# A 16x16 transpose of the identity between the down products and the next pair's gate and up products of an expert layer

## The chip, the cores and the metric

The kernel runs on one core of one Trainium2 chip. The metric is the device time of one execution in microseconds (us). Before the change the median of three runs is 2702.27 us (2701.55 to 2703.72).

## The reference, cut to what matters

The reference is one layer of a diffusion backbone over 2048 latent tokens of 1024 channels with 256 context tokens: a mixing sub-layer (a convolution beside an mLSTM scan), then a routed layer of 16 experts, then a final RMSNorm. The change lies in the routed layer alone. Each expert picks its 256 best tokens and runs them through a gated product of width 1408:

```python
aff = softmax(hs @ w_router, over experts)
g, idx = top_k(aff, cap)                    # cap = 256 tokens for each of 16 experts
xe = hs[idx]
a = einsum('ecd,edf->ecf', xe, w_gate)      # gate
u = einsum('ecd,edf->ecf', xe, w_up)        # up
ye = einsum('ecf,efd->ecd', silu(a) * u, w_down) * g[..., None]
out = segment_sum(ye, idx)                  # added back at the tokens' rows
```

All inputs are float32.

## The kernel before, in words

Each float32 operand of a large product is split into a rounded high part and a low part (`whi`, `wlo` for the weights, `xh`, `xl` for the tokens, `dhi`, `dlo` and `hh`, `hl` for the down product), and each product is the sum of three matmuls: high by high, high by low, low by high. ScalarE (ACT) makes the high parts and VectorE (DVE) the low parts, in lines 93, 97, 1075 and 1077.

The loop over the experts `e` (line 1157) holds a loop over `pr`, six pairs of 128-wide blocks of the 1408 hidden columns (the sixth pair has one block). For each pair the gate and up weights are loaded and split, and then for each block one PSUM tile `psx` takes the gate and the up product of 256 tokens: 2 x 8 x 3 = 48 matmuls with a moving operand of 256 columns, lines 1192 to 1194. A full pair so has 96 of them, called a run below, and the sixth pair 48. `psx` comes from the pool `pmm`, which has three buffers. ACT and DVE turn it into `hh` and `hl`.

The down products are one pair behind: after the gate and up products of pair `pr`, line 1212 issues those of the pair before, 24 matmuls (12 for a sixth pair) with 512 columns each into four PSUM accumulators `ac`, lines 1117 to 1119. Then, after pair 1, `xgather` finds the next expert's tokens with 16 small bf16 matmuls of 4 columns into `pi` (line 1013), and after pair 3 `xprep` transposes those tokens: 16 float32 transposes of 128x128 into `ptx` (line 1055), in four groups of four, which a planner spreads over the following pairs.

The order on each engine comes from a planner that works with modelled times. `keep_in_program_order` pins one instruction behind the last one written before it on the same engine. TensorE (PE) has a row of its own for the loading of stationary operands (PEld).

Of the kernel before, what the change touches and what calls it, by code (L numbers as in the profile page):

```python
# [8 lines left out]
F32 = mybir.dt.float32  # L9
# [10 lines left out]
P = 128  # L20
# [5 lines left out]
NE = 16  # L26
# [12 lines left out]
def kernel(ctx, tc, x, c, cx, c_ctx, w_mod, b_mod, g_norm1, g_norm2, w_in, w_out, conv_w, conv_b,  # L39
                       gate_b, g_head, w_router, w_gate_e, w_up_e, w_down_e, g_final, out):  # L40
    nc = tc.nc
    V, S, G, T = nc.vector, nc.scalar, nc.gpsimd, nc.tensor
# [20 lines left out]
    ident = con.tile([P, P], F32, name="ident")  # L63
# [20 lines left out]
    def load_w(src, rows, cols):  # L84
        raw = wrawp.tile([P, rows, cols], F32, name="wraw", tag="wraw")
        nc.sync.dma_start(raw, src)
        return raw
# [56 lines left out]
    def pool(st, name, bufs, **kw):  # L144
        return st.enter_context(tc.tile_pool(name=name, bufs=bufs, reuse_waits="tile", **kw))
# [3 lines left out]
    pmm = pool(left, "p1mm", 4, space=PSUM)  # L149
# [99 lines left out]
    for q in range(4):  # L249
        pmf = psm.tile([P, 512], F32, name="pm", tag="sm")  # L250
        pm = pmf[:, 0:8].rearrange("p (r i s) -> p r i s", r=2, i=2)
        for r in range(2):
            pr = pmm.tile([P, 512], F32, name="pr", tag="mm")
# [157 lines left out]
    def wstat(w, i, h, ntok):  # L411
        hi, lo = w
        his, los = h
        ps = pmm.tile([P, 512], F32, name="ps", tag="mm")
        for k in range(KD):
            wh = hi[:, k, i * P:(i + 1) * P]
            T.matmul(ps[:, :ntok], wh, his[k], start=k == 0, stop=False)  # L417
            T.matmul(ps[:, :ntok], wh, los[k], start=False, stop=False)  # L418
            T.matmul(ps[:, :ntok], lo[:, k, i * P:(i + 1) * P], his[k], start=False, stop=k == KD - 1)  # L419
        return ps  # L420
# [127 lines left out]
    for blk in range(4):  # L548
        KT = wk.tile([P, NH, 512], F32, name="KT", bufs=1)
        for j in range(2):  # L550
            w = wtile(2048 + j * 256)
            if blk == 0:
                for i in range(2):
                    ps = wstat(w, i, hc, NCTX)
                    S.activation(KTc[:, j * 2 + i, :], ps[:, :NCTX], AF.Copy)
            for i in range(2):
                ps = wstat(w, i, h, 512)
# [6 lines left out]
        for j in range(2):  # L564
            w = wtile(2560 + j * 256)
            if blk == 0:
                for t in range(2):
                    ps = hstat(w, hc, t)
                    V.tensor_copy(V1c[t][:, j * 2:j * 2 + 2, 0:P], ps[:, :256].rearrange("p (h v) -> p h v", h=2))
            for t in range(4):  # L570
                if j == 0:
                    V.memset(V1s[t][:, :, P:P + 1], 1.0)
                ps = hstat(w, h, t)
# [8 lines left out]
        for j in range(2):  # L582
            w = wtile(1536 + j * 256)
            for i in range(2):
                ps = wstat(w, i, h, 512)
# [60 lines left out]
        for j in range(2):  # L646
            mod_tile(j)
            w = wtile(3072 + j * 256)
            for t in range(4):
                so = wl.tile([P, 256], F32, name="so", bufs=2)  # L650
                ps = hstat(w, h, t)
# [4 lines left out]
        for j in range(2):  # L656
# [3 lines left out]
            for i in range(2):  # L660
                ps = wstat(w, i, h, 512)
# [5 lines left out]
            for i in range(2):  # L667
                ct = j * 2 + i
                ps = wstat(w, i, h, 512)
# [12 lines left out]
            for i in range(2):  # L682
                ct = j * 2 + i
                y = ys[i]
                ps = wstat(w, i, h, 512)
# [311 lines left out]
    with tc.tile_pool(name="xw", bufs=2, reuse_waits="tile") as xraw, tc.tile_pool(name="xh", bufs=2, reuse_waits="tile") as xhi, \  # L997
# [5 lines left out]
        def xgather(e):  # L1003
            oh = wk.tile([P, P, 16], BF16, name="oh", bufs=1)
            if e == 1:
                V.tensor_copy(oh[:, 0, 0:1], xp[1].bitcast(F32)[:, KD - 1, 0:1])
            for js in ((slice(0, 8), slice(8, 16)) if e == 0 else (slice(0, 16),)):
                n = js.stop - js.start
                V.tensor_tensor(oh[:, :, js], ix[:, :, js], AH[:, e, js].unsqueeze(1).to_broadcast([P, P, n]),
                                op=ALU.is_equal)  # L1010
            pi = ptr.tile([P, 512], F32, name="pi", tag="tr")
            for j in range(16):
                T.matmul(pi[:, 0:4], oh[:, :, j], RB[:, e, j], start=j == 0, stop=j == 15)
            idx = wk.tile([P, 2], I32, name="idx", bufs=3)
            with nc.allow_low_precision(reason="whole numbers up to 2047"):
                V.tensor_reduce(idx[:, ::-1], pi[:, 0:4].rearrange("p (h f) -> p h f", f=2), axis=AX.X, op=ALU.add)
            gxs = [wk.tile([P, XW], F32, name="gx", bufs=2) for _ in range(2)]
            for hf_ in range(2):
                G.indirect_dma_start(out=gxs[hf_], out_offset=None, in_=XN,
                                     in_offset=bass.IndirectOffsetOnAxis(ap=idx[:, hf_:hf_ + 1], axis=0))  # L1020
            if e == 0:
                warm = pmm.tile([P, 512], F32, name="warm", tag="mm")
                for j in range(20):
                    tc.keep_in_program_order(T.matmul(warm, oh[:, :, j % 16], ix[:, 0:32].rearrange("p a j -> p (a j)"),
                                                      start=True, stop=True))
            gg = wk.tile([P, 2], F32, name="gg", bufs=2)
            return gxs, gg, idx
# [74 lines left out]
        def early_store(t, a, fr):  # L1102
            V.scalar_tensor_tensor(a, a, fr, gfb, op0=ALU.mult, op1=ALU.mult)
            nc.sync.dma_start(out[t * P:(t + 1) * P, :], a)
# [48 lines left out]
                G.indirect_dma_start(out=out, out_offset=rows(e, hf_), in_=ar, in_offset=None)  # L1153

        xp = xprep(0, xgather(0))
        pend, held = [], []
        for e in range(NE):
            xh, xl, gg, idx = xp
            idx_of[e] = idx
            accs = None  # L1160
            nxt = None
            for pr in range(npair):
                n = 2 if pr < npair - 1 else NFT - 2 * (npair - 1)
                f0 = pr * 2
                ws = []
                for src in (w_gate_e, w_up_e):
                    raw = load_w(src[0, e][:, f0 * P:(f0 + n) * P].rearrange("(k p) n -> p k n", p=P), KD, n * P)
                    if e == 0 and pr == 0:
                        ws.append(split_w(raw, KD, n * P, thr[:, 0:1], nhalf))
                    elif e == 0 and pr == 1 and not ws:  # L1170
                        ws.append(split_w(raw, KD, n * P, xl.bitcast(F32)[:, 5, 0:1]))
                    else:
                        ws.append(split_w(raw, KD, n * P))
                dw = wsplit_d(w_down_e[0, e][f0 * P:(f0 + n) * P, :].rearrange("(i p) n -> p i n", p=P), n,
                              gg[:, 0:1] if e == 0 and pr < 2 else None,
                              xl.bitcast(F32)[:, KD - 1, 0:1] if e == 0 and pr < 2 else None)
                if e == 0 and pr == 0:
                    other_places(xl.bitcast(F32)[:, KD - 1, 0:1])
                for rec in held:
                    early_store(*rec)  # L1180
                held = []
                if e >= NE - 2 and pr:
                    cuts = ((0, 2, 4, 6, 8, 10), (10, 12, 14, 16, 16, 16))[e - NE + 2]
                    held = [early_load(t) for t in range(cuts[pr - 1], cuts[pr])]
                hts = []
                for i in range(n):
                    ps = pmm.tile([P, 2, 2 * P], F32, name="psx", tag="mm")
                    for m_ in range(2):
                        hi, lo = ws[m_]
                        for k in range(KD):  # L1190
                            wh = hi[:, k, i * P:(i + 1) * P]
                            T.matmul(ps[:, m_], wh, xh[:, k], start=k == 0, stop=False)  # L1192
                            T.matmul(ps[:, m_], wh, xl[:, k], start=False, stop=False)  # L1193
                            T.matmul(ps[:, m_], lo[:, k, i * P:(i + 1) * P], xh[:, k], start=False, stop=k == KD - 1)  # L1194
                    sgt = wk.tile([P, 2 * P], F32, name="sgt", bufs=2)
                    S.activation(sgt, ps[:, 0], AF.Silu)  # L1196
                    V.tensor_tensor(sgt, ps[:, 1], sgt, op=ALU.mult)  # L1197
                    if e == 0 and pr == 0 and i == 0:
                        wk.tile([P, 16], F32, name="gaph", bufs=1)
                    hh = wk.tile([P, 2 * P], F32R, name="hh", bufs=4)  # L1200
                    S.activation(hh, sgt, AF.Copy)  # L1201
                    hl = wk.tile([P, 2 * P], F32R, name="hl", bufs=4)
                    V.tensor_sub(hl, sgt, hh.bitcast(F32))
                    hts.append((hh, hl))
                last = pr == npair - 1
                for rec in held:
                    early_scale(rec, hts[-1][0].bitcast(F32)[:, 0:1])
                if pend and not (e == NE - 1 and last):
                    pe, pxp, paccs, ppr, plast = pend.pop()
                    if paccs is None:  # L1210
                        paccs = [pac.tile([P, 512], F32, name="ac", tag="ac") for _ in range(4)]
                    down(paccs, ppr)
                    if plast:
                        finish(pe, pxp, paccs)
                    else:
                        accs = paccs
                pend.append((e, xp, accs, ([f0 + i for i in range(n)], hts, dw), last))
                if e == NE - 2 and last:
                    old_rows(e)
                if pr == 1 and e + 1 < NE:  # L1220
                    gth = xgather(e + 1)
                if pr == 3 and e + 1 < NE:
                    nxt = xprep(e + 1, gth)
            if nxt is not None:
                xp = nxt
# [51 lines left out]
```

## Time and profile before

| what | value |
|---|---|
| median of three runs | 2702.27 us |
| time of the profiled execution | 2698.35 us |
| its span, first to last instruction | 2696.3 us |
| TensorE busy (PE) | 97% of the span |
| VectorE, ScalarE, GpSimd busy | 59%, 43%, 11% |
| gate and up matmuls (lines 1192 to 1194) | 8448, about 788 us busy each line |
| down matmuls (lines 1117 to 1119) | 2112, about 275 us busy each line |
| mean granted TensorE clock | 0.989 of full speed |

A matmul's duration in the profile reaches from its issue to its modelled end, and consecutive matmuls overlap. What a stream of them costs is therefore read from the distance between starts, or from the length of a stretch divided by the number of matmuls in it. In the window view the count in parentheses also takes in the two to four neighbours that reach into the stretch.

### The profile page before, as it was taken

To read this page: it belongs to the slowest core of one execution; us is meant where nothing else is said; L and a number is where in the kernel's file an instruction comes from. 1 tells how busy PE (TensorE), PEld (TensorE's weight loads), DVE (VectorE), ACT (ScalarE), POOL (GpSimd) and SP (SyncE) were. 2 spreads that over 40 slices of the span, in tenths; PEclk is the share of its full clock that TensorE was granted. 3 is DMA by queue.
4 is the path that set the end of the run, shared out by engine and by line. 5 is a ranking of instruction groups with operands and counts; after the bars stand their busy time and mean duration, and the time that the engine had idled before them with its cause. 6 is when DMAs were issued, how large, how long until landed. Compare 5 with 4: busy or idle time off the path is not lost.

```text
span 2696.3 us, 42922 instructions
## 1 busy us (share of the span) xinstructions
PE 2615.3 (97%) x17570; PEld 2365.0 (88%) x17570; DVE 1584.3 (59%) x2570; ACT 1155.3 (43%) x1723; POOL 301.0 (11%) x345
## 2 busy tenths in 40 slices
PE   8999999999999999689999999999999999999997
PEld 4988888888878888579999999999999999999987
DVE  5356454554575665566566556656655665665684
ACT  3243333422534444354444444444444444444553
POOL 1010000000111111210011011001101100110231
PEclk9999999999999999889999999999999999999999
DMA  8444554645656655165666666666666666666894
GB/s 271 135 147 148 170 165 147 196 129 156 204 183 206 208 183 172 64 219 188 205 217 208 200 209 219 189 208 214 209 202 208 219 191 206 214 210 202 276 318 166
DMA packets 382532, 524.57 MB, mean 195 GB/s; under 512 B 15072, under 2 KB 322736, under 8 KB 380288
## 3 DMA queue, kind: packets, MB, share of 16 engines
q1 hardware_dynamic: 327968, 437.96, 50.0%
q10 hardware_dynamic: 43792, 46.55, 5.1%
q0 software_dynamic: 10576, 37.32, 5.0%
q8 instruction: 138, 2.26, 0.3%
q14 instruction: 58, 0.48, 0.1%
HBM read 449.05 MB, written 72.61 MB: 193 GB/s over the span
## 4 chain that ended last, share of the span: by engine, by line
PE 63%; DMA 3%; DVE 2%; issue 2%; ACT 0%; POOL 0%; POOLq 0%; DVEq 0%; SPq 0%; ACTq 0%
PE psx L1192 12%; PE psx L1194 11%; PE psx L1193 11%; PE ac L1117 6%; PE ac L1119 6%; PE ac L1118 6%; PE po L730 2%; PE po L732 2%; PE po L731 2%; DMA pk<-PK 1%; PE ptx L1055 1%; PE pl L766 1%; PE pb L514 1%; PE pa L510 1%; DMA ACC<-yv,idx 1%
## 5 line engine op out<-in xcount | busy, mean ns | idle before, releaser
L1192 PE MATMUL psx<-xh,whi 128*128 128x256 f32 x2816 | 788.9, 281 | 1.6 <-ACT whi L93 1.5
L1193 PE MATMUL psx<-xl,whi 128*128 128x256 f32 x2816 | 786.7, 280 | 0.9 <-DVE xl L1064 0.9
L1194 PE MATMUL psx<-xh,wlo 128*128 128x256 f32 x2816 | 787.5, 280 | 0.0
L97 DVE TENSOR_TENSOR wlo<-wraw,whi 128x2048 fp32r<-128x2048 f32 x248 | 532.0, 2156 | 307.8 <-ACT whi L93 304.7
L93 ACT ACTIVATE whi<-wraw 128x2048 fp32r<-128x2048 f32 x248 | 446.7, 1804 | 373.3 <-PE psx L1193 112.1
L1194 PEld LDWEIGHTS psx<-xh,wlo 128*128 128x128 f32 x2816 | 535.3, 190 | 0.1
L1193 PEld LDWEIGHTS psx<-xl,whi 128*128 128x128 f32 x2816 | 530.5, 188 | 3.3 <-DVE xl L1064 1.4
L1192 PEld LDWEIGHTS psx<-xh,whi 128*128 128x128 f32 x2816 | 528.7, 188 | 4.1 <-ACT whi L93 1.7
L1117 PE MATMUL ac<-dhi,hh 128*128 128x512 f32 x704 | 276.2, 392 | 0.0
L1118 PE MATMUL ac<-dlo,hh 128*128 128x512 f32 x704 | 274.7, 390 | 0.0
L1119 PE MATMUL ac<-dhi,hl 128*128 128x512 f32 x704 | 273.3, 390 | 0.0
L1077 DVE TENSOR_TENSOR dlo<-draw,dhi 128x2048 fp32r<-128x2048 f32 x96 | 202.9, 2114 | 114.2 <-ACT dhi L1075 114.2
L418 PE MATMUL ps<-hlo,whi 128*128 128x512 f32 (+1 forms) x672 | 259.6, 387 | 0.0
L419 PE MATMUL ps<-hhi,wlo 128*128 128x512 f32 (+1 forms) x672 | 259.0, 386 | 0.0
L417 PE MATMUL ps<-hhi,whi 128*128 128x512 f32 (+1 forms) x672 | 258.6, 388 | 0.0
L1147 POOL DMA_INDIRECT ACC<-yv,idx x28 | 82.8, 2956 | 1124.1 <-DVE yv L1142 1012.6
L1075 ACT ACTIVATE dhi<-draw 128x2048 fp32r<-128x2048 f32 x96 | 170.2, 1772 | 69.7 <-PE ac L1119 67.6
L1201 ACT ACTIVATE hh<-sgt 128x256 fp32r<-128x256 f32 x176 | 73.2, 417 | 263.0 <-DVE sgt L1197 263.0
L1196 ACT ACTIVATE sgt<-psx 128x256 f32<-128x256 f32 x176 | 65.4, 372 | 228.0 <-PE psx L1194 227.9
L1119 PEld LDWEIGHTS ac<-dhi,hl 128*128 128x128 f32 x704 | 132.1, 188 | 27.8
L428 PE MATMUL ps<-whi,hhi 128*128 128x256 f32 x544 | 156.0, 287 | 0.0
L429 PE MATMUL ps<-wlo,hhi 128*128 128x256 f32 x544 | 154.9, 285 | 0.0
(411 smaller groups left out, 3901.8 us busy)
## 6 DMA issues: line engine op xcount, KB each, us to landing
wraw<-in_w_gate_e_dram SPq DMA_DIRECT2D x80, 1024.0 KB, 6.2
wraw<-in_w_up_e_dram SPq DMA_DIRECT2D x80, 1024.0 KB, 5.5
draw<-in_w_down_e_dram SPq DMA_DIRECT2D x80, 1024.0 KB, 6.1
wraw<-in_w_in_dram SPq DMA_DIRECT2D x56, 1024.0 KB, 5.5
pk<-PK SPq DMA_DIRECT2D x16, 1284.0 KB, 7.7
xt<-in_x_dram SPq DMA_DIRECT2D x32, 512.0 KB, 5.5
wraw<-in_w_mod_dram SPq DMA_DIRECT2D x16, 1024.0 KB, 6.8
wm<-in_w_mod_dram SPq DMA_DIRECT2D x8, 1024.0 KB, 12.0
```

What stands on the lines that cost most here:

```text
L93: S.activation(hi, raw, AF.Copy)
L97: V.tensor_sub(lo, raw, hi.bitcast(F32))
L417: T.matmul(ps[:, :ntok], wh, his[k], start=k == 0, stop=False)
L418: T.matmul(ps[:, :ntok], wh, los[k], start=False, stop=False)
L419: T.matmul(ps[:, :ntok], lo[:, k, i * P:(i + 1) * P], his[k], start=False, stop=k == KD - 1)
L1077: V.tensor_sub(lo, raw, hi.bitcast(F32))
L1117: T.matmul(ac, hhs, dh[:, i, sl], start=f == 0, stop=False)
L1118: T.matmul(ac, hhs, dl[:, i, sl], start=False, stop=False)
L1119: T.matmul(ac, hls, dh[:, i, sl], start=False, stop=f == NFT - 1)
L1192: T.matmul(ps[:, m_], wh, xh[:, k], start=k == 0, stop=False)
L1193: T.matmul(ps[:, m_], wh, xl[:, k], start=False, stop=False)
L1194: T.matmul(ps[:, m_], lo[:, k, i * P:(i + 1) * P], xh[:, k], start=False, stop=k == KD - 1)
```

## The change

One transpose is added after the down products of a pair, 94 times in all: after every pair but the first of expert 0 and the last of expert 15. It reads 16 partitions by 16 columns of the constant identity and writes 16x16 elements of the `psx` tile that the next pair's first block is to use; that tile is now taken from the pool here and handed over in the list `ahead_ps`. The first matmul of the next pair starts its accumulation anew and overwrites what the transpose wrote. `keep_in_program_order` pins the transpose behind the last PE instruction written before it: the last down product, or after pair 1 the last `pi` matmul. After pair 3 it stands ahead of `xprep`.

```diff
-        pend, held = [], []
+        pend, held, ahead_ps = [], [], []
...
-                    ps = pmm.tile([P, 2, 2 * P], F32, name="psx", tag="mm")
+                    ps = ahead_ps.pop() if ahead_ps else pmm.tile([P, 2, 2 * P], F32, name="psx", tag="mm")
...
                 if pr == 1 and e + 1 < NE:
                     gth = xgather(e + 1)
+                if (e or pr) and not (e == NE - 1 and last):
+                    ps = pmm.tile([P, 2, 2 * P], F32, name="psx", tag="mm")
+                    tc.keep_in_program_order(T.transpose(ps[:16, 0, :16], ident[:16, :16], ident[:16, :16]))
+                    ahead_ps.append(ps)
                 if pr == 3 and e + 1 < NE:
                     nxt = xprep(e + 1, gth)
```

## Rows read from the trace of the kernel before

**Rows 1.** The page: span, and TensorE's busy time, share and instructions.

```profile
span 2696.3 us, 42922 instructions
PE 2615.3 (97%) x17570; PEld 2365.0 (88%) x17570; DVE 1584.3 (59%) x2570; ACT 1155.3 (43%) x1723; POOL 301.0 (11%) x345
```

**Rows 2.** Windows: stretch, length, engines' busy us (instructions), granted clock, DMA share, GB/s.

```profile
1250.00:2650.00 1400.00, 1396.43 (x10225) 1313.82 (x10224) 867.32 (x958) 664.19 (x753) 163.44 (x94) 1.00 0.68 218
```

**Rows 3.** Windows, PE alone: gate and up runs of experts 4, 5, 15.

```profile
1543.98:1555.29 11.31, 11.31 (x98) 1.00 0.61 203
...
1575.77:1586.74 10.97, 10.97 (x99) 1.00 1.02 340
1592.20:1603.51 11.31, 11.31 (x98) 1.00 0.51 161
1609.31:1617.48 8.17, 8.17 (x75) 1.00 0.64 210
...
1626.59:1632.13 5.54, 5.54 (x51) 1.00 0.97 302
1669.87:1681.26 11.39, 11.39 (x100) 1.00 0.97 326
...
2617.45:2628.76 11.31, 11.31 (x98) 1.00 0.91 312
```

**Rows 4.** Timeline, PE: start, duration, line, operands; down products into a run.

```profile
1591.97 0.39 PE L1119 MATMUL ac<-dhi,hl 128*128 128x512 f32 x1
1592.20 0.28 PE L1192 MATMUL psx<-xh,whi 128*128 128x256 f32 x1
```

**Rows 5.** Timeline, PE: down products, four transposes of 128x128, then a run.

```profile
1608.72 0.40 PE L1119 MATMUL ac<-dhi,hl 128*128 128x512 f32 x1
1608.95 0.60 PE L1055 MATMUL ptx<-ident,gx 128*128 128x128 f32 x4
1609.31 0.37 PE L1192 MATMUL psx<-xh,whi 128*128 128x256 f32 x1
1609.52 0.28 PE L1193 MATMUL psx<-xl,whi 128*128 128x256 f32 x1
```

**Rows 6.** Timeline, PE: the sixteen matmuls of `xgather`, then a run.

```profile
1574.76 1.15 PE L1013 MATMUL pi<-Cb,oh 128*128 128x4 bf16 x16
1575.77 0.36 PE L1192 MATMUL psx<-xh,whi 128*128 128x256 f32 x1
1575.97 0.28 PE L1193 MATMUL psx<-xl,whi 128*128 128x256 f32 x1
```

**Rows 7.** Timeline, PE: a transpose of 16 rows among 256-column matmuls (earlier stage).

```profile
709.60 0.28 PE L428 MATMUL ps<-whi,hhi 128*128 128x256 f32 x1
709.81 0.23 PE L399 MATMUL pM<-ident,rm 16*128 16x16 f32 x1
709.97 0.39 PE L429 MATMUL ps<-wlo,hhi 128*128 128x256 f32 x1
710.19 0.28 PE L430 MATMUL ps<-whi,hlo 128*128 128x256 f32 x1
```

**Rows 8.** Timeline, PE: the same transpose behind a 512-column matmul.

```profile
716.61 0.39 PE L418 MATMUL ps<-hlo,whi 128*128 128x512 f32 x1
716.93 0.23 PE L399 MATMUL pM<-ident,rm 16*128 16x16 f32 x1
```

**Rows 9.** Lines L399, L338: weight loads; count, ns min/median/max, when, shape.

```profile
L399 PEld LDWEIGHTS pM<-ident,rm x8: 132/133/134, 168.7 to 728.6; 16*128 16x128 f32 x8
...
L338 PEld LDWEIGHTS pu<-ident,uc x2: 86/87/88, 158.9 to 159.0; 128*16 128x16 f32 x2
```

**Rows 10.** Expert 0's first run: a start after idling (timeline), what follows (window).

```profile
1168.45 0.39 PE L1193 MATMUL psx<-xl,whi 128*128 128x256 f32 x1 [0.42 <-DVE xl L1064]
...
1169.02:1181.47 12.45, 12.41 (x110) 1.00 0.91 324
```

**Rows 11.** Window, PE: 288 matmuls of 256 columns in the input projection.

```profile
83.28:117.83 34.55, 34.55 (x290) 1.00 0.49 151
```

## The prediction

> **What bounds the kernel now.** I read the page first: TensorE is busy 97% of the span [rows 1]. Then the window over the experts: PE is busy 1396.43 of 1400 us at a granted clock of 1.00, the 2.4 GHz level [rows 2]. Nothing that other engines or transfers do ends a wait there; a microsecond in the expert layer is won or lost only in how densely PE's own stream runs. Since durations of pipelined matmuls overlap, I next cut the stream into its runs and divided each by its matmuls [rows 3].
>
> The reader is to see two paces for the same 96 matmuls. A run that follows the down products directly [rows 4] takes 11.31 us, 0.1178 us a matmul; so in expert 4 for pairs 0 and 3, and in expert 15. A run that follows the transposes of `xprep` [rows 5] goes at 0.1134: 71 matmuls in 8.17 us with a slow first step of 0.21, and 48 in 5.54. After the `pi` matmuls both occur: 10.97 us in expert 4, 11.39 in expert 5, alternating from expert to expert. In 10.97 the first step takes 0.20 [rows 6] and the other 95 take 10.77, 0.1134 each. The clock is 1.00 in all of them and the DMA share does not sort them (0.51 and 0.91 in long runs, 1.02 in a short one), so neither is the cause. What a run keeps is the pace into which it starts. The short pace is worth 0.0044 us a matmul, 0.42 us a run.
>
> So the question is whether the added transpose starts each run at the short pace, and what it costs on the way.
>
> **Does it set the pace?** The trace has no 16x16 transpose here. Its two neighbours are the 128x128 transposes, after which all runs of pairs 4 and 5 are short, and starts of a PE that stood empty: after 0.42 us of waiting in expert 0, the next 12.45 us hold about 110 matmuls, 0.113 each [rows 10]. Against it: in the input projection 288 matmuls of the same shape take 0.120 each [rows 11], and nothing resets them, the 16-row transposes there included [rows 7]; and some `pi` starts fail. I take it that the pace is set, since both neighbours in this stage agree.
>
> **What does the transpose cost?** It uses 16 rows of the array, and the trace has transposes of 16 rows, L399, eight of them with the same times. Behind a 512-column matmul L399 starts 0.32 us after it [rows 8], where a down product is followed after 0.23 [rows 4]: +0.09. The next full matmul starts 0.16 after it and the second one 0.22 later [rows 7], where a step is 0.12: +0.10. Loading is not hidden on either side of it. The Trainium skill says otherwise ("TensorE: Matmul & The Clock Gate", section "Step-by-step: what each phase is for"): a weight load is pulled ahead of running matmuls if it goes to the background buffer or to rows that don't conflict. By that rule the transpose would fit almost wholly under its neighbours; L399 disagrees.
>
> L399 loads 128 columns, the new one 16. A load of 16 columns is 0.046 us shorter than L399's [rows 9], so I take its own slot as 0.16 - 0.05 = 0.11 us; ends: 0.16 (loading not shorter at all) and 0.07 (twice the difference).
>
> **The sum**, by what the 94 transposes stand in front of:
>
> - 48 full runs directly after down products (three for each of experts 1 to 14, two at expert 0's end, four in expert 15). Run before: 11.31. After: first step 0.22, 95 x 0.1134 = 10.77, and 0.02 to settle (in rows 5, 8.17 - 0.21 over 70 steps is 0.0003 a step above pace): 11.01. Saved 0.30; transpose 0.09 + 0.11 = 0.20. The down products after a short run lose 0.01 (estimate). Net gain 0.09 each, 4.3 in all.
> - 8 long runs after `pi` (expert 0 and the odd ones to 13): 11.39 to 11.01, less 0.20: 0.18 each, 1.4.
> - 7 short runs after `pi`: 10.97 to 11.01, plus 0.20: -0.24 each, -1.7.
> - 30 places where the transposes of `xprep` lie at the same boundary and the run is short already: 0.09 + 0.11, and the first 128-wide load, now open instead of under a down product, between 0 and 0.10, taken as 0.06: -0.26 each, -7.8.
> - The last pair, 48 matmuls: 48 x 0.0044 = 0.21 saved against 0.20 + 0.10: -0.1.
>
> Together 4.3 + 1.4 - 1.7 - 7.8 - 0.1 = **-3.9 us**, a loss. The profiled execution took 2698.35 us (span 2696.3 and 2.05 around it) and would take 2702.3; it lies 3.9 below the median of the runs, so the median would be 2702.27 + 3.9 = **2706 us**. With the slot at 0.07 it is 94 x 0.04 = 3.8 better, at 0.16 it is 4.7 worse, and the open load adds 1.5 either way: 2701 to 2712 for this case alone.
>
> Nothing else moves. The transpose waits for what the run's first matmul waited for, a `psx` buffer whose readers ended during the 5.5 us of down products (24 x 0.23 [rows 4]), and it needs no transfer. Behind it on PE stand the run and the `ptx` transposes; ACT and DVE get `psx` earlier or later by a few tenths and have slack (664 and 867 of 1400 us busy [rows 2]). SP's and POOL's queues are not touched. The pin behind the last `pi` matmul costs nothing: that matmul ran directly ahead of the run anyway [rows 6]. The planner may place the groups of `ptx` differently; as each costs the same wherever it stands, I price that at zero, with 1 us either way.
>
> **The rivals.**
>
> *The transpose slips in like the others* (faster). If its load hides under the last down product, as the first of the four `ptx` does (0.23 after the down product, and the four take 0.36 to the run's start, the last of them about 0.03 [rows 5]), a place costs 0.03 instead of 0.20: 48 x 0.26 = 12.5, 8 x 0.35 = 2.8, 7 x -0.07 = -0.5, and 30 places between -0.03 and -0.11 = -0.9 to -3.3. Gain 11.5 to 14: 2690. For it: both kinds are float32 transposes. Against: all eight L399. It decides by the start of the transpose, 0.23 or 0.32 after the last down product. The rule of the skill quoted above is this rival's.
>
> *The pace is not reset* (slower). Then the long runs keep 0.1178 and pay: 48 x (0.20 + 0.10) = 14.4; the long ones after `pi` lose 8 x 0.23 = 1.8, the short ones up to 7 x 0.65 = 4.6, and the 30 places 7.8. Loss 28.6: 2731. For it: the projection's unmoved 0.120 and the failing `pi` starts. Against: every start from transposes or from an empty PE in this stage. It decides by the third to tenth step of a run, 0.118 or 0.113. The Trainium skill's one distance for each width (the same page, "Back-to-back issue gap": N / 2.4 + 2.5 ns, 109 ns for 256 columns) knows no pace that a start could change, and by it only the cost is left; the two paces of rows 3 speak against that rule.
>
> *The pace is reset for part of the pairs only.* The pace depends on what a run reads too: `xh` alternates between two buffers with the expert, and so do the starts after `pi`. The weights rotate through three buffers, and behind `ptx` only pairs 4 and 5 were seen. If pairs 0 and 3, which share the third combination, stay long, 31 places lose 0.40 each, 12.4 more: 2718. Against: expert 0's first pair, with those buffers, is short after its waits [rows 10].
>
> *The transpose stands elsewhere.* It writes the tile that the run's first matmul overwrites and is pinned behind the down products, so only `ptx` groups can come between, and those reset the pace themselves; the time stays that of the forecast.
>
> **How the numbers follow.** The forecast has 0.68, the faster rival 0.20, no reset 0.08, part of the pairs 0.04. Something over 0.2%, 5.4 us, is what a measurement can tell from no change here: 2696.9 and 2707.7 are the bounds. The forecast's own range of 2701 to 2712 lies about a third above 2707.7. Slower: 0.08 + 0.04 + 0.22 = 0.34; faster: 0.20; same: 0.46. The forecast and the faster rival together hold 0.88, so the range reaches from 2688 to 2713.
>
> **What would show it.** Right: the new transpose starts about 0.32 us after the last down product, the run 0.11 after it, the second step is 0.22, and full runs of all pairs then take 11.0 us. Each of these is a term; a transpose at 0.23 means the faster rival, runs that still take 11.3 or 11.4 the slower one. It would also be wrong if PE began to wait in the expert layer, which would show as idle time before the new transpose.

## The result

The change makes the kernel slower: 2724.47 us (2719.17 to 2726.34, four runs) against 2702.99 us for the kernel before, a ratio of 1.0079 with a 95% interval of 1.0066 to 1.0092. The forecast was 2706, no change or a slight loss, with a range up to 2713. The profiled execution took 2719.17 us, 20.8 more than that of the kernel before.

The page of the changed kernel: span, and TensorE's busy time, to be read beside [rows 1].

```profile
span 2717.1 us, 43095 instructions
...
PE 2639.6 (97%) x17664; PEld 2365.5 (87%) x17664; DVE 1585.9 (58%) x2570; ACT 1157.8 (43%) x1723; POOL 308.7 (11%) x345
```

TensorE got 94 matmuls more and is busy 24 us longer; no other engine changed by more than 8 us. So the time is in PE's own stream, and there it has to be looked for in the runs. Windows of PE in the changed kernel (stretch, length, busy us and instructions, granted clock, DMA share, GB/s): expert 3's pairs 0, 1, 2, 3, then expert 4's pair 2 and the two parts of its pair 4. They answer to [rows 3].

```profile
1453.96:1465.37 11.41, 11.41 (x97) 1.00 0.58 188
1468.29:1479.70 11.41, 11.41 (x97) 1.00 0.96 288
1486.34:1497.35 11.01, 11.01 (x98) 1.00 0.99 326
1503.01:1514.01 11.00, 11.00 (x98) 1.00 0.54 160
1581.75:1593.17 11.42, 11.42 (x97) 1.00 0.95 321
1616.32:1624.47 8.15, 8.15 (x74) 1.00 0.62 213
1624.83:1627.86 3.03, 3.03 (x29) 1.00 0.03 5
```

Two lengths of run are there again, 11.0 and 11.4, and every one of these full runs has the new transpose directly ahead. A start behind it costs 0.1 us more than a start behind down products, so a long run now takes 11.41 where it took 11.31. From expert 1 to expert 14 pairs 0 and 1 are long everywhere, pair 2 is long in the even experts, and pair 3 with it (in expert 1 too). The granted clock is 1.00, the 2.4 GHz level, in all of them.

Now the same boundary twice at close range. The timeline of PE in the changed kernel (start, duration, line, operands) ahead of a long run, expert 3's pair 0:

```profile
1453.53 0.39 PE L1119 MATMUL ac<-dhi,hl 128*128 128x512 f32 x1
1453.85 0.18 PE L1224 MATMUL psx<-ident 16*16 16x16 f32 x1
1453.96 0.39 PE L1192 MATMUL psx<-xh,whi 128*128 128x256 f32 x1
1454.18 0.28 PE L1193 MATMUL psx<-xl,whi 128*128 128x256 f32 x1
```

and ahead of a short one, its pair 3:

```profile
1502.58 0.39 PE L1119 MATMUL ac<-dhi,hl 128*128 128x512 f32 x1
1502.89 0.18 PE L1224 MATMUL psx<-ident 16*16 16x16 f32 x1
1503.01 0.39 PE L1192 MATMUL psx<-xh,whi 128*128 128x256 f32 x1
1503.23 0.28 PE L1193 MATMUL psx<-xl,whi 128*128 128x256 f32 x1
```

The transpose, line 1224, starts 0.32 and 0.31 us after the last down product, the run 0.11 and 0.12 after it, the second matmul 0.22 later. To a hundredth of a microsecond the two starts can hardly be told apart, and yet the run goes on at 0.118 us a matmul in one case and 0.1134 in the other. The trace keeps starts in nanoseconds, and there they differ: in experts 1 to 13 every long run of pairs 0, 1 and 3 starts 109 or 110 ns after the transpose and its second matmul 225 or 226 ns later, every short run of pair 3 starts after 111 ns and its second matmul 221 or 222 ns later.

At the 30 boundaries that hold transposes of the next tokens, the planner put the new one ahead of them after pair 3 and behind them after pair 4. Timeline of PE, changed kernel, expert 3:

```profile
1519.24 0.39 PE L1119 MATMUL ac<-dhi,hl 128*128 128x512 f32 x1
1519.56 0.18 PE L1224 MATMUL psx<-ident 16*16 16x16 f32 x1
1519.67 0.66 PE L1055 MATMUL ptx<-ident,gx 128*128 128x128 f32 x4
1520.08 0.37 PE L1192 MATMUL psx<-xh,whi 128*128 128x256 f32 x1
...
1537.05 0.60 PE L1055 MATMUL ptx<-ident,gx 128*128 128x128 f32 x4
1537.58 0.18 PE L1224 MATMUL psx<-ident 16*16 16x16 f32 x1
1537.69 0.38 PE L1192 MATMUL psx<-xh,whi 128*128 128x256 f32 x1
1537.91 0.28 PE L1193 MATMUL psx<-xl,whi 128*128 128x256 f32 x1
```

From the last down product to the run it is 0.84 us after pair 3, where it was 0.59 [rows 5]: 0.25 lost. Behind the four, the new transpose starts 0.53 after the first of them and the run's second matmul 0.33 after it, 0.86 in all, where it was 0.57 at the boundary of [rows 5]: 0.29 lost.

Where the 20.8 us of the profiled executions went, with these lengths (a loss is positive):

| places | each | sum |
|---|---|---|
| 41 full runs behind down products that stayed long (11.31 to 11.41, transpose 0.09 + 0.11) | 0.30 | 12.3 |
| 7 of them that became short (11.31 to 11.00, the same transpose) | -0.11 | -0.8 |
| 8 runs behind `pi` that became short (11.39 to 11.01, transpose 0.18) | -0.20 | -1.6 |
| 7 runs behind `pi` that became long (10.97 to 11.42, transpose 0.18) | 0.63 | 4.4 |
| 30 places at transposes of tokens | 0.27 | 8.1 |
| second part of pair 4, now long (2.95 to 3.03), experts 0 to 13 | 0.08 | 1.1 |
| last pair of expert 15 | 0.31 | 0.3 |
| together | | 23.8 |

From the first matmul of expert 1 to the first of expert 14, where PE waits for nothing, the stream takes 1245.90 us instead of 1226.24, 19.7 more. The remaining -3 lies in expert 14's pair 4. Who waited there for whom (us, times, longest), in the waits of PE in the kernel before and then in the changed kernel:

```profile
PE ptx L1055 <- DVE xf L1063: 3.6, 1, 3.6
```

```profile
PE ptx L1055 <- DVE xf L1063: 1.8, 1, 1.8
```

and the stretch behind that pause, in the windows of PE before and after:

```profile
2565.93:2568.56 2.63, 2.63 (x17) 0.62 1.02 375
```

```profile
2586.48:2588.16 1.68, 1.68 (x17) 1.00 0.99 405
```

The wait is 1.8 us shorter. In the kernel before the 17 instructions behind it ran at a granted clock of 0.62 on the mean, so partly at the 1.2 GHz level, after PE had been idle for those 3.6 us; in the changed kernel the clock stays at 1.00, the 2.4 GHz level, and they take 0.95 us less. Together 2.75.

### The profile page after: what moved, and what is told of

Its sections match the earlier page's. It is cut to its first block, busy times and chain, and to the rows that moved or that the text cites. A ratio compares the mean times of both kernels' runs of the same rounds, so it can differ in the third digit from the quotient of the medians.

```text
span 2717.1 us, 43095 instructions
## 1 busy us (share of the span) xinstructions
PE 2639.6 (97%) x17664; PEld 2365.5 (87%) x17664; DVE 1585.9 (58%) x2570; ACT 1157.8 (43%) x1723; POOL 308.7 (11%) x345
## 4 chain that ended last, share of the span: by engine, by line
PE 64%; DMA 3%; DVE 2%; issue 2%; ACT 0%; POOL 0%; POOLq 0%; DVEq 0%; SPq 0%; ACTq 0%
PE psx L1192 12%; PE psx L1193 11%; PE psx L1194 11%; PE ac L1118 6%; PE ac L1119 6%; PE ac L1117 6%; PE po L730 2%; PE po L732 2%; PE po L731 2%; DMA pk<-PK 1%; PE ptx L1055 1%; PE pl L766 1%; PE pb L514 1%; PE pa L510 1%; DMA ACC<-yv,idx 1%
```

## The experiments

The question was why the transpose set the short pace in some places and not in others. Three theories were on the table: **phase** (a few nanoseconds at the start of a run decide its pace, and these come from the stream before), **what the run reads** (buffers and addresses decide, pair by pair), and **kind** (full transposes reset the pace, an emptied array does not). The table gives the outcome for experts 1 to 14: S a short run, L a long one; pair 4 is cut in two by transposes of tokens.

| kernel | pair 0 | 1 | 2 | 3 | 4 | 5 | us, median |
|---|---|---|---|---|---|---|---|
| before | L | L | S in even experts | L | S/S | S | 2702.99 |
| changed, 16x16 | L | L | S in odd | S in odd from 3 on | S/L | S | 2724.47 |
| e1: the same again | L | L | S in odd | S in odd from 3 on | S/L | S | 2723.71 |
| e2: 128x128 | L | S | L | S | L/S | S | 2704.34 |
| e3: 128x16 | L | L | S in 1, 2 and odd from 5 on | L | S/S | S | 2710.87 |
| e4: 16x32 | L | S | S | L | S/L | S | 2718.44 |
| e5: 128x128 after pairs 0, 2 | L | L | S in even | S | S/S | S | 2700.64 |
| e6: 16x16, not after pairs 3, 4 | L | L | S in odd | S in odd | S/S in even, L/L in odd | S | 2717.92 |
| e7: 16x20 | S | S | L | S | S/L | S | 2711.09 |
| e8: 16x16, buffers moved | L | L | L | L | L/L | L | 2750.27 |
| e9: before, buffers moved | L | L | L | L | L/L | L | 2721.76 |
| e10: 16x18 | S | S | L | S | S/L | S | 2714.42 |
| e11: 128x128 after pair 2 | L | L | S in even | L | S/S | S | 2703.31 |
| e12: 16x20 after pairs 0, 2, 5 | S | S | S in even | S | S/S | S | 2697.33 |

Runs with a pause in expert 14 are left out of the table. The kernel before was timed beside each group; its medians there were 2702.01 (e1 to e4), 2701.43 (e5 to e8) and 2701.61 (e9 to e12).

### Is the pattern chance? (e1)

No edit.

> The changed kernel once more, unaltered. In its profile the transpose costs what was forecast (0.32 us behind a down product, 0.11 to the run, 0.22 for the first step), but 41 of the 48 full runs behind down products kept the long pace (0.118 us a matmul): all of pairs 0 and 1, and pair 3 wherever pair 2 was long. Theory 'what the run reads' (buffers and program decide): the same runs are long and short again, pair by pair, and the time is 2717 to 2726 us. Theory 'phase' (a few ns at the start decide, and these come from what went before, waits for transfers included): the pattern may differ between executions, and the spread of the four times, 2719 to 2726, would be that.

2723.71 us, and from expert 1 on the same pattern, run by run, in another execution; experts 1 to 13 again take 1245.90 us. The windows of expert 3's pairs 0 and 2:

```profile
1457.18:1468.59 11.41, 11.41 (x98) 1.00 0.57 189
1489.56:1500.57 11.01, 11.01 (x98) 1.00 0.99 333
```

There the pace is not drawn by lot in each execution: PE hardly waits for anything, so its stream repeats. That fits both "what the run reads" and a phase that the stream itself carries along. Expert 0's first run is another matter. It begins after waits for other engines, no added transpose stands ahead of it, and here it is long, where it was short in the kernel before and in the changed one. The window that answers to that of [rows 10], also behind a wait of 0.42 us:

```profile
1171.39:1184.32 12.93, 12.89 (x110) 1.00 0.92 320
```

The same number of matmuls takes 12.93 us where it took 12.45. Over the twelve profiles with the buffers as in the kernel before, this run is short in seven and long in five.

### The transpose's size (e2, e3, e4)

```diff
-T.transpose(ps[:16, 0, :16], ident[:16, :16], ident[:16, :16])
+T.transpose(ps[:, 0, :P], ident, ident)                          # e2
+T.transpose(ps[:16, 0, :P], ident[:, :16], ident)                # e3
+T.transpose(ps[:32, 0, :16], ident[:16, :32], ident[:16, :16])   # e4
```

> The same transpose at the same 94 places, but of the whole 128x128 identity. It uses all 128 rows, so if the 0.09 us behind the down product comes from the change to 16 rows it starts 0.23 us after the last down product and the run follows after 0.03. Theory 'full transposes reset the pace, emptied arrays do not': runs of all pairs become short, 11.0 us, gain 48 x 0.26 + 8 x 0.35 - 30 x 0.03 to 0.11 = about 12 us, 2690 us. Theory 'what the run reads': pairs 0 and 1 stay long, 29 runs of the 48 gain nothing and pay about 0.13, so the sum is 19 x 0.26 + 2.8 - 29 x 0.13 - 0.5 - 3.3 = about 0, 2703 us. Theory 'phase': a mixture that differs from that of the changed kernel.

2704.34 us, 1.0009 of before (0.9999 to 1.0018). Timeline of PE at expert 3's pair 1, the row of its weight load (PEld) here and the one ahead of pair 0 in the changed kernel, and the windows of e2's pairs 0, 1 and 3:

```profile
1464.00 0.40 PE L1119 MATMUL ac<-dhi,hl 128*128 128x512 f32 x1
1464.23 0.27 PE L1224 MATMUL psx<-ident 128*128 128x128 f32 x1
```

```profile
1464.00 0.14 PEld L1224 LDWEIGHTS psx<-ident 128*128 128x128 f32 x1
```

```profile
1453.85 0.08 PEld L1224 LDWEIGHTS psx<-ident 16*16 16x16 f32 x1 [0.35 <-issue]
```

```profile
1450.12:1461.51 11.39, 11.39 (x99) 1.00 0.60 194
1464.26:1475.25 10.99, 10.99 (x98) 1.00 0.95 279
...
1498.67:1509.65 10.98, 10.98 (x99) 1.00 0.56 175
```

With all 128 rows the load starts at 1464.00, together with the last down product, and the transpose 0.23 us after that: the load is hidden. With 16 rows load and transpose start together at 1453.85, 0.32 after the down product. So the 0.09 goes away with the full transpose. "Kind" falls: a full transpose leaves pair 0 and pair 2 long, and the first part of pair 4, which stands behind five full transposes here, went from short to long. "What the run reads" in the strict form falls too, since pair 1 reads the same buffers as before and is short.

> The same places, a transpose of all 128 rows but 16 columns of the identity (weights 128x16, moving 128 columns). It tells rows from size: if the cost comes from using 16 rows, it starts 0.23 us behind a down product as the 128x128 one does, about 2690 to 2703 us with the pace as in that run; if it comes from any small stationary operand, it starts 0.32 us behind it, and the time is that of the changed kernel or worse. On the pace the theories say the same as for the 128x128 transpose.

2710.87 us, 1.0032 (1.0021 to 1.0043). Ahead of expert 3's pair 1 the last down product starts at 1471.01, and the transpose 0.23 us after it:

```profile
1471.24 0.27 PE L1224 MATMUL psx<-ident 128*16 128x128 f32 x1
```

So a narrow stationary operand does not cost the 0.09. Nor do few moving columns: the bf16 matmuls of `xgather`, 128 rows with 4 moving columns, start at 1574.76 in the kernel before [rows 6], 0.23 after this down product:

```profile
1574.53 0.39 PE L1119 MATMUL ac<-dhi,hl 128*128 128x512 f32 x1
```

What is left is the 16 rows. But pairs 0, 1 and 3 are all long, at 11.39 with the entry. Against e2 only the stationary operand is narrower.

> The same places, a transpose of 16 rows by 32 columns instead of 16 by 16: one size changed. The load of 16 more columns lengthens it by about 0.005 to 0.01 us, so its cost alone would add 94 x 0.008 = 0.7 us. Theory 'phase': that shift of some ns changes which runs are long and short in a way that the buffers cannot explain, pairs 0 and 1 included, and the time can move either way by some 10 us. Theories 'what the run reads' and 'an emptied array does not reset': the same runs stay long, 2718 to 2727 us.

2718.44 us, 1.0058 (1.0041 to 1.0075), some 6 us less than the changed kernel. The transpose's slot grew from 0.11 to 0.12, and pair 1, long everywhere with 16 columns, became short in all experts, pair 2 likewise, while pair 3 became long. Windows of expert 3's pairs 1 to 3:

```profile
1470.85:1481.85 11.00, 11.00 (x97) 1.00 0.96 283
1488.51:1499.52 11.01, 11.01 (x98) 1.00 0.98 327
1505.18:1516.59 11.41, 11.41 (x97) 1.00 0.46 143
```

That is what "phase" said and the others did not: some 7 ns more ahead of a run change the pace of whole pairs, in both directions.

### Two nanoseconds (e7, e10)

```diff
-T.transpose(ps[:16, 0, :16], ident[:16, :16], ident[:16, :16])
+T.transpose(ps[:20, 0, :16], ident[:16, :20], ident[:16, :16])   # e7
+T.transpose(ps[:18, 0, :16], ident[:16, :18], ident[:16, :16])   # e10
```

> All 94 places, 16 rows by 20 columns, between the changed kernel's 16 and the 32 that made pair 1 short everywhere. The transpose gets about 2 ns longer. Theory 'phase': 2 ns are enough to change the pace of whole pairs, in one direction or the other; theory 'what the run reads': nothing changes, pairs 0 and 1 long, pair 2 alternating, 2723 us.

2711.09 us, 1.0037 (1.0022 to 1.0053), 13 less than the changed kernel, by four columns. The transpose's rows in both profiles (engine, count, ns min/median/max, when, shape), first the changed kernel's, then e7's:

```profile
L1224 PE MATMUL psx<-ident x94: 178/179/182, 1198.7 to 2688.3; 16*16 16x16 f32 x94
```

```profile
L1224 PE MATMUL psx<-ident x94: 180/181/182, 1199.4 to 2679.5; 16*20 16x16 f32 x94
```

Two nanoseconds longer; and the windows of expert 3's pairs 0 to 3 in e7:

```profile
1453.02:1464.02 11.00, 11.00 (x97) 1.00 0.59 197
1466.96:1477.96 11.00, 11.00 (x97) 1.00 0.97 284
1484.61:1496.02 11.41, 11.41 (x97) 1.00 0.95 316
1501.66:1512.65 10.99, 10.99 (x97) 1.00 0.46 139
```

Pairs 0, 1 and 3 are short in all experts, pair 2 is long in all. "What the run reads" alone is refuted: nothing was changed that the run reads.

> All 94 places, 16 rows by 18 columns, half way to the 20 that made pairs 0, 1 and 3 short and pair 2 long everywhere. The slot grows by about 1 ns. If about a nanosecond decides, the pattern is that of 16 columns, that of 20 or a third one, with whole pairs at one pace; the time follows the count of short steps: some 2711 us with the pattern of 20, 2723 with that of 16.

2714.42 us from two runs (2710.84 and 2718.01), with the pattern of 20 columns; experts 1 to 13 take 1235.36 us here and in e7, so what the two medians differ by lies elsewhere. The transpose of 18 columns lasts 181 ns as that of 20 does. Equal durations go with equal patterns; duration and a column count above 16 are not told apart by these two runs, but by those below in which the transpose ahead of a run stays the same and its pace changes (e5 and e11).

### What the runs read (e8, e9)

```diff
-wk.tile([P, 40], F32, name="gapx", bufs=1)
+wk.tile([P, 72], F32, name="gapx", bufs=1)
```

e8 is the changed kernel with this edit, e9 the kernel before with it.

> The changed kernel with every later buffer of the expert layer (xh, xl among them) moved by 128 bytes in each partition: an unused spacer of 40 columns made 72. The PE stream is the same. Theory 'what the run reads' (addresses): the pattern of long and short runs changes. Theory 'phase': the pattern stays, pairs 0 and 1 long, pairs 2 and 3 short in the odd experts, 2723 us.

2750.27 us (2748.07 and 2752.47). No run is short any more, wherever it starts. The first part of expert 3's pair 4, which took 8.15 in the changed kernel:

```profile
1528.78:1537.23 8.45, 8.45 (x74) 1.00 0.57 198
```

So the placement of the buffers matters after all, in another way than I had put it: with this one there is no short pace to be had. "Phase" was wrong here in saying that the pattern stays.

> The kernel before, without any added transpose, with the spacer of 72 columns instead of 40. The changed kernel with that spacer took 2750 us, kept the long pace in every run, whatever stood ahead of it, and its down products went from 0.227 to 0.232 us. If where the operands lie decides whether there is a short pace at all, the same holds without the transposes: no step at the short pace, 2703 of them lost at 0.0044 (11.9 us) and 2112 down products at 0.005 (10.6): 2724 us. If the loss of the short pace needs the transposes, it stays near 2702.

2721.76 us (2723.35 and 2720.18), 20 more than before, without any added transpose. Windows of e9, expert 3: the 24 down products after pair 3, the first part of pair 4.

```profile
1517.38:1522.99 5.61, 5.61 (x27) 1.00 0.43 127
1523.34:1531.79 8.45, 8.45 (x74) 1.00 0.61 217
```

The 71 matmuls behind the token transposes took 8.17 [rows 3] and take 8.45 here. The 24 down products take 5.61 us, 0.234 each, where 0.227 was the rule. The expected 2724 from the count of lost short steps is nearly met. So the short pace needs two things: of the two placements tried, the one that the kernel has, and a start at the right moment.

### The term for the 30 places, and fewer transposes (e6, e5, e11)

```diff
-if (e or pr) and not (e == NE - 1 and last):
+if (e or pr) and not (e == NE - 1 and last) and (pr not in (3, 4) or e == NE - 1):   # e6
+if (e or pr) and pr in (0, 2) and not (e == NE - 1 and last):                        # e5
+if pr == 2 and e < NE - 1:                                                            # e11
```

e5 and e11 use the 128x128 transpose of e2, e6 the 16x16 one.

> The 16x16 transpose at 64 places only: not after pairs 3 and 4 of experts 0 to 14, where the transposes of the next tokens stand anyway. The term of the forecast for those 30 places was 0.26 us each, 7.8 in all; in the profile of the changed kernel it is (0.09 + 0.11 + 0.06) x 15 in front of the token transposes and (0.18 + 0.11 + 0.02) x 15 behind them, 8.5. If the pace of the other runs stays as in the changed kernel: 2723 - 8.5 = 2715 us. By theory 'phase' the pace of other runs may change too, mostly of pair 4's second part and pair 0, up to 1.4 and 6 us either way.

2717.92 us (2714.26 to 2720.56), 6.5 less than the changed kernel, where 8.5 was expected with an unchanged pattern. The pattern did change: pair 4, which starts behind token transposes alone as in the kernel before, is long in the odd experts. Windows of its first part in experts 3 and 4:

```profile
1519.68:1528.13 8.45, 8.45 (x75) 1.00 0.66 214
1615.72:1623.87 8.15, 8.15 (x75) 1.00 0.64 207
```

Seven experts lose 0.30 there, about 2 us, which is about the difference. It also shows that the token transposes do not reset the pace by themselves: the same four stand ahead of both runs.

> The 128x128 transpose of the identity only after pairs 0 and 2, 31 places, in front of the runs of pairs 1 and 3, which were short in the run with it at all 94 places; the other boundaries are as in the kernel before. Theory 'phase' (what a run starts at is fixed by the few ns at its start, and these by the stream before it): it can't be told from one run what the others do, but if the two starts depend mainly on what stands directly ahead, pairs 1 and 3 are short again: 30 x 0.27 = 8 us gained, 2694 us, pairs 4 and 5 short as in the kernel before; if the earlier stream matters as well, some of them fall back and it is 2694 to 2705 us.

2700.64 us, 0.9999 (0.999 to 1.0009): pair 3 short as hoped, pair 1 long, although in e2 it was short behind the same transpose.

> The 128x128 transpose after pair 2 of experts 0 to 14 alone, 15 places. In the run with it after pairs 0 and 2 pair 3 was short in experts 0 to 14 and pair 1 long, so pair 1 paid for nothing. If pair 3 stays short: 15 x (11.31 - 10.99 - 0.03 - 0.02) = 3.8 us gained, 2698 us. If pair 3's pace hangs on the transpose after pair 0 as well, it is 15 x 0.13 = 2 us slower than before.

2703.31 us, 1.0006 (0.9997 to 1.0015): without the transpose after pair 0, pair 3 is long again. Windows of pair 3 of expert 3 in e5 and in e11:

```profile
1502.40:1513.39 10.99, 10.99 (x98) 1.00 0.57 176
```

```profile
1500.97:1512.36 11.39, 11.39 (x98) 1.00 0.55 174
```

The same instruction stands ahead of the same run in both, and the same buffers are read. What differs in the program lies more than two runs earlier, and it arrives as nanoseconds: in experts 1 to 13 the transpose starts 235 ns after the last down product in e5 and 230 or 231 in e11. The start that counts is thus not set by the instruction ahead alone; it is handed on from run to run. It does not come from the layer's beginning, though: in e1 expert 0's first run was long instead of short, and the pattern from expert 1 on was the same.

### The transpose only where it paid (e12)

```diff
-if (e or pr) and not (e == NE - 1 and last):
+if (e or pr) and pr in (0, 2, 5) and not (e == NE - 1 and last):
...
-T.transpose(ps[:16, 0, :16], ident[:16, :16], ident[:16, :16])
+T.transpose(ps[:20, 0, :16], ident[:16, :20], ident[:16, :16])
```

> The transpose of 16 rows by 20 columns only after pairs 0, 2 and 5, in front of the runs that were long in the kernel before and short in the run with it at all places (pairs 1, 3, 0): 48 places at 0.20 + 0.10 us, 46 runs at 95 x 0.0044 = 0.42 less. If all three pairs are short: 46 x 0.10 = 5 us gained, 2697 us. If they are short only with the others in place, up to 48 x 0.30 = 14 us slower, 2716 us.

2697.33 us, 0.9987 of before (0.9978 to 0.9997), which is 3.5 us less (4.3 between the medians); there are 46 such places, not 48. Expert 3's pairs 0, 1 and 3:

```profile
1449.71:1460.71 11.00, 11.00 (x98) 1.00 0.63 203
1463.65:1474.65 11.00, 11.00 (x98) 1.00 0.97 282
...
1498.17:1509.17 11.00, 11.00 (x97) 1.00 0.49 146
```

All three pairs are short, in front of each a transpose at 0.20 us, and 5 us were expected for that. Experts 1 to 13, with 39 of the places, take 1222.34 us instead of 1226.24: 0.10 gained at each. It is the forecast's sum for those places, with its pace.

## Why the prediction was wrong

**The bound was right.** PE's stream sets the time; nearly everything that was gained or lost is in the length of its runs and in the steps between them. The forecast said that nothing ends a wait there; its own window holds one pause of 3.6 us in expert 14, and that pause and what follows it moved by 2.75 us.

**The price of the transpose was right.** The forecast had 0.09 behind a down product, 0.11 for its own slot and 0.10 in the run's first step, read from a 16-row transpose of another stage; the changed kernel shows 0.09, 0.11 and 0.10. The 30 places at token transposes were put at 0.26 and cost 0.25 and 0.29. The rival by which its load is hidden is out for 16 rows: the transpose starts 0.32 us after the down product, together with its load. The Trainium skill ("TensorE: Matmul & The Clock Gate", "Step-by-step: what each phase is for") has loads pulled ahead when they go to the background buffer or to rows that don't conflict; e2 and e3 with 128 rows agree, with a start 0.23 us after the down product, and the 16-row load was not pulled ahead. Which of the two conditions it misses, no run here shows.

**The step that failed is "Does it set the pace?".** I took it that the pace is set, since the runs behind 128x128 transposes and behind an empty PE were all short. Those were many observations of few starts: those behind transposes repeat in every expert at the same moment of the same stream, and the empty PE of [rows 10] was one start in one execution, which came out long in e1. What looked like a property of transposes was that moment: in e2 a full transpose leaves pairs 0 and 2 long, in e6 the same four token transposes stand ahead of long and of short runs. With the change, 41 of the 48 runs at stake stayed long, and the 7 runs behind `pi` that had been short were lost. The failing `pi` starts, alternating from expert to expert with the same instructions ahead, were the row that spoke of a phase, and I gave them too little weight. My rival "the pace is not reset" came nearest: of its price of 28.6 us for all places, 21.5 came, three quarters. Its mechanism was not quite right either, as 15 runs did turn short, 8 of them behind `pi`. The rival that resets part of the pairs rested on what a run reads; that matters (e8, e9), but it named pairs 0 and 3, and 0 and 1 stayed long.

**The sum itself holds where its condition does.** In e7 pairs 0, 1 and 3 are short as the forecast wanted, and of the full runs only pair 2 is long: 15 runs at 11.41 instead of 11.01 add 6 us to 2706, and the second part of pair 4, long too, about 1, which gives 2713; measured 2711.09.

What stays open is why a nanosecond or two at the start and 128 bytes of placement should both act on TensorE's pace. No run here looks at that, and which operand's place counts was not tried.

## What to carry to other kernels

Where a saturated stream shows two paces for the same instructions, first ask what fixes the pace, with a run that shifts the stream by a few nanoseconds and one that moves the operands, before a start from one place is taken as a cure for another: a pattern that repeats in every iteration is one observation. A transpose of 16 rows among matmuls of 128 rows cost about 0.3 us here where the run behind it kept its pace (11.41 instead of 11.31, and 0.20 for the transpose), since its load did not lie under the matmul before it; one with all 128 rows, whose load did, cost about 0.1 us (e2: 0.03 to the run's start and 0.08 in its first step).

## What was not expected of the hardware

The pace of 96 matmuls turns on 2 ns: with a transpose of 181 instead of 179 ns pairs 0 and 1 of every expert from 1 to 14, and pair 3 wherever it was long, went from 0.118 to 0.1134 us a matmul, and pair 2 of the odd experts the other way, 13 us in all (e7). And moving the layer's buffers by 128 bytes in each partition cost the kernel before 20 us (e9), in the down products (0.234 instead of 0.227 us) as in the gate and up products, with the same instructions in the same order.
